# State-space exponents: the mask moved from a product of its own into the free rows of the sums' product

## The chip, the cores and the metric

The kernel runs on one core of one Trainium2 chip. The metric is the time of one execution on the device, in microseconds; the median of three runs is given with the lowest and the highest. The profiles show one execution each, with the engines TensorE (PE for the matmuls, PEld for loading their weights), VectorE (DVE), ScalarE (ACT), GpSimd (POOL) and SyncE (SP), which issues the transfers.

## The reference, cut to what matters

The program is one layer of a decoder trunk over 1024 positions of width 1024: a mixing sub-layer (stick-breaking attention beside a Mamba-2 state-space mixer), cross-attention to 256 memory rows, and a feed-forward. The change lies in the state-space mixer, in chunks of 128 positions, 4 groups of 8 heads:

```python
a_cs = jnp.cumsum(a_dt, axis=-1)
tril = jnp.tril(jnp.ones((SSM_CHUNK, SSM_CHUNK), dtype=bool))
decay = jnp.exp(jnp.where(tril, a_cs[..., :, None] - a_cs[..., None, :], -jnp.inf))
cb = jnp.einsum('bclgn,bcsgn->bcgls', cc, bc)
y_diag = jnp.einsum('bcgls,bcgels,bcsgep->bclgep', cb, decay, xc)
```

Within a chunk, position l takes from position s, at or before it, `C_l . B_s` times the exponential of the difference of two running sums. Above the diagonal the decay is zero. The states of the chunks before and a running state per group complete the output.

## The kernel before, in words

The stage in question comes behind the attention (its pools open at `with ExitStack() as p3`). It goes over 32 units, n = 0 to 31: group g = n // 8, chunk c = n % 8. Four functions handle a unit: `prep` makes its decay matrix and weighted inputs, `states` carries the running state on, `outp` forms the output and its variance, `flip` transposes it; `branch` then multiplies four finished chunks by a weight matrix. `prep` runs two units ahead of `outp`. Between them stand pieces of the memory's projections for the later cross-attention (`memory`, `mem_quanta`), which fill the first units, and `branch_load`, which splits weights. A scheduler with a model of the engines sets each engine's order when the program is built; each engine then takes its own instructions strictly in that order, waiting on semaphores. The program's rows are named by tile: `dec` is the accumulator of the exponents (two buffers), `seg` (its tile reads `s` in the profile) the decay matrix of 8 heads by 128 positions, `cb` is C B^T of four chunks.

The exponent of head h, key position s and query position l is a difference of sums, and one matmul makes it for four heads. The stationary operand is `keyrows` (128 rows by 512 positions): rows 0 to 7 and 32 to 39 hold the key-side sums of the 8 heads in two parts, rows 64 and 65 hold ones. The moving operand is `colrows` (two tiles in turn): rows 0 to 7 and 32 to 39 hold the identity over the heads, which picks each head's sum; rows 64 and 65 are loaded per unit with the query-side sums. The other 110 rows of both are zero. The mask comes from a matmul of its own into the same accumulator, ahead of it: identity times `bar`, a matrix of -2^120 above the diagonal and zero elsewhere. ScalarE then takes the exponential (L1022, two halves of four heads), and VectorE multiplies all 8 heads by C B^T (L1023, 128x1024).

The attention ends at about 1105 us of the span, and the stage's constants are made there: `identr` and `bar` by VectorE (L953, L958; the mask itself earlier by GpSimd, L956 and L957), the zeros of `colrows` and `keyrows` by GpSimd (L964), the head identities by VectorE (L967), the ones by GpSimd (L969). C B^T is computed once per four chunks in `open_four` (L995) and copied out by ScalarE (L997).

Around the change: L1045 scales the running state and L1046 adds to it; L1028 weights the inputs; L1062, L1068, L1076 and L1077 form the output; L1080 takes its variance on ScalarE, GpSimd makes 1/sqrt of it (L163, L164), and L1082 scales by it; L1095 is the transpose. L1073 is the product of the decay matrix with the inputs. L94 and L97 are the helpers that split a tensor into a high and a low part; L100 to L102 the three matmuls of a split product.

Of the kernel before, what the change touches and what calls it, by code (L numbers as in the profile page):

```python
# [8 lines left out]
F32 = mybir.dt.float32  # L9
F32R = mybir.dt.float32r  # L10
BF16 = mybir.dt.bfloat16
AF = mybir.ActivationFunctionType
ALU = mybir.AluOpType
# [3 lines left out]
P = 128  # L17
# [9 lines left out]
NG, GH = 4, 8  # L27
FFN = 2816
NF = FFN // P
ML = 256  # L30
FILL_LEFT, FILL_RIGHT = 96, 224


@with_exitstack
def hybrid_block(ctx, tc, a, out, dbg=None):
    nc = tc.nc
    V, A, G, T = nc.vector, nc.scalar, nc.gpsimd, nc.tensor

    def pool(stack, name, bufs=1, space=None, side=None):
        kw = {} if space is None else {"space": space}  # L40
        if side is not None:
            kw["side"] = side
        if space is not DRAM:
            kw["reuse_waits"] = "tile"
        return stack.enter_context(tc.tile_pool(name=name, bufs=bufs, **kw))
# [3 lines left out]
    def mk(pl, shape, dt, tag, bufs=None):  # L49
        uid[0] += 1  # L50
        kw = {} if bufs is None else {"bufs": bufs}
        return pl.tile(shape, dt, tag=tag, name=f"{tag}_{uid[0]}", **kw)
# [43 lines left out]
    def lo_of(o, i, hi, eng=V):  # L96
        eng.tensor_tensor(o, i, hi.bitcast(F32), ALU.subtract)  # L97
# [21 lines left out]
    ident = mk(cp, [P, P], F32, "ident")  # L119
# [129 lines left out]
    with ExitStack() as pa:  # L249
# [52 lines left out]
        with ExitStack() as p1:  # L302
            tt = pool(p1, "tcomb", 6)
            ep = pool(p1, "early", 4)
# [145 lines left out]
            for i, s in enumerate(steps_v + steps_z):  # L450
                if i == 4:
                    load_z()
                if i % 3 == 0 and i < 12:
                    c = i // 3
# [114 lines left out]
        with ExitStack() as p1:  # L569
# [3 lines left out]
            t4 = pool(p1, "t4b", 6)  # L573
# [144 lines left out]
        with ExitStack() as p2:  # L718
# [190 lines left out]
            for m in range(NM):  # L909
                h, half = m // 2, m % 2  # L910
                hp, r = m // 4, m % 4
# [4 lines left out]
                if m >= NM - 5:  # L916
                    n = -(-len(late) // (NM - m))
# [10 lines left out]
    with ExitStack() as p3:  # L928
        AHEAD = 2
        gb = pool(p3, "gbs", 2)  # L930
        sm = pool(p3, "smp", 2)
        t4 = pool(p3, "s4p", 3)
        t2 = pool(p3, "s2p", 9)
        ep = pool(p3, "exps", 1)
# [7 lines left out]
        def v3(t, n=HD):  # L942
            return t.rearrange("p (h d) -> p h d", d=n)
# [5 lines left out]

        identr = mk(ep, [P, P], F32R, "identr")
        V.tensor_copy(identr, ident)  # L953
        bar = mk(ep, [P, 4, P], F32R, "bar")
        tri = mk(t4, [P, GH, P], F32, "s4")
        G.memset(tri, 0.0)  # L956
        G.affine_select(tri, tri, [[0, GH], [1, P]], ALU.is_ge, -(2.0 ** 120), base=0, channel_multiplier=-1)  # L957
        V.tensor_copy(bar, tri[:, 0:4, :])  # L958
        NROW = 2
        HEADS, ONES = (0, 32), 64  # L960
        colrows = [mk(ep, [P, GH, P], F32R, f"colrows{i}") for i in range(NROW)]
        keyrows = [mk(ep, [P, HALF], F32R, f"keyrows{i}") for i in range(2)]
        for t in colrows + keyrows:
            G.memset(t.bitcast(F32), 0.0)  # L964
        for t in colrows:
            for r in HEADS:
                V.tensor_copy(t[r:r + GH], ident[r:r + GH, r:r + GH].unsqueeze(2).to_broadcast([GH, GH, P]))  # L967
        for t in keyrows:
            G.memset(t[ONES:ONES + 2].bitcast(F32), 1.0)  # L969

        def open_four(g, q):

            cols = slice(q * HALF, (q + 1) * HALF)
            d = four[g, q] = {}
            d["keys"] = keyrows[(2 * g + q) % 2]
            for j in range(2):
                nc.sync.dma_start(d["keys"][HEADS[j]:HEADS[j] + GH].bitcast(F32), key_d[j, g * GH:(g + 1) * GH, cols])
            bfm = d["bfm"] = mk(sm, [P, HALF], F32, "bfm", bufs=1)
            nc.sync.dma_start(bfm, bf_d[g][:, cols])
            cfm = d["cfm"] = mk(sm, [P, HALF], F32, "cfm", bufs=1)  # L980
            nc.sync.dma_start(cfm, cf_d[g][:, cols])
            btm = mk(sm, [P, 4, P], F32, "btm", bufs=1)
            nc.sync.dma_start(btm, bt_d[g][cols, :].rearrange("(c p) n -> p c n", p=P))
            bh = d["bh"] = mk(sm, [P, 4, P], F32R, "bh")
            bl = d["bl"] = mk(sm, [P, 4, P], F32R, "bl")
            hi_sb(bh, btm, "a")
            lo_of(bl, btm, bh)
            ch = d["ch"] = mk(sm, [P, HALF], F32R, "ch")
            cl = d["cl"] = mk(sm, [P, HALF], F32R, "cl")
            hi_sb(ch, cfm, "a")  # L990
            lo_of(cl, cfm, ch)
            pm = mk(ps, [P, 4, P], F32, "dec", bufs=2)
            for ci in range(4):
                cs = slice(ci * P, (ci + 1) * P)
                T.matmul(pm[:, ci, :], bfm[:, cs], cfm[:, cs], start=True, stop=True)  # L995
            cb = d["cb"] = mk(sm, [P, 4, P], F32, "cb")
            A.activation(cb, pm, AF.Copy)  # L997

        def prep(n):

            g, c = divmod(n, NCH)
            q, ci = divmod(c, 4)
            if c == 0:
                grp[g] = {}
            if ci == 0:
                open_four(g, q)
            f4 = four[g, q]
            cs = slice(ci * P, (ci + 1) * P)
            d = chk[n] = {}
            rows_ = slice(c * P, (c + 1) * P)  # L1010
            cr = colrows[n % NROW]
            for j in range(2):
                nc.sync.dma_start(cr[ONES + j:ONES + j + 1].bitcast(F32), sum_d[j:j + 1, g * GH:(g + 1) * GH, rows_])
            xs = d["xs"] = mk(t2, [P, HALF], F32, "s2")
            nc.sync.dma_start(xs, xs_d[g][rows_, :])
            seg = d["seg"] = mk(t4, [P, GH, P], F32, "s4")
            for j in range(2):
                hs = slice(4 * j, 4 * j + 4)
                pe = mk(ps, [P, 4, P], F32, "dec", bufs=2)
                T.matmul(pe, identr, bar, start=True, stop=False)  # L1020
                T.matmul(pe, f4["keys"][:, cs], cr[:, hs, :], start=False, stop=True)
                A.activation(seg[:, hs, :], pe, AF.Exp)  # L1022
            V.tensor_tensor(seg, seg, f4["cb"][:, ci, :].unsqueeze(1).to_broadcast([P, GH, P]), ALU.mult)  # L1023
            d["ch"], d["cl"] = f4["ch"][:, cs], f4["cl"][:, cs]
            if c < NCH - 1:
                d["bh"], d["bl"] = f4["bh"][:, ci, :], f4["bl"][:, ci, :]
                xw = mk(t2, [P, HALF], F32, "s2")
                G.tensor_tensor(v3(xw), v3(xs), bc(wm, c, g), ALU.mult)  # L1028
                xwh = d["xwh"] = mk(t2, [P, HALF], F32R, "s2r", bufs=4)
                xwl = d["xwl"] = mk(t2, [P, HALF], F32R, "s2r", bufs=4)  # L1030
                hi_sb(xwh, xw, "a")
                lo_of(xwl, xw, xwh)
# [192 lines left out]
        for n in range(AHEAD):  # L1225
            prep(n)
# [16 lines left out]
        for n in range(-AHEAD, NN + 4):  # L1243
# [15 lines left out]
            if 0 <= n - 2 < NN:  # L1259
                flip(n - 2)  # L1260
                if (n - 2) % 4 == 3:
                    g, c = divmod(n - 2, NCH)
# [24 lines left out]
    with ExitStack() as p4:  # L1287
# [15 lines left out]
        for k in range(KT):  # L1303
            oh.append(mk(op, [P, S], F32R, f"oh{k}"))
            ol.append(mk(op, [P, S], F32R, f"ol{k}"))
            for half in range(2):
                sl = slice(half * HALF, (half + 1) * HALF)
                t = mk(t2, [P, HALF], F32, "m2")
# [55 lines left out]
    t4 = pool(xt4, "t4x", 3)  # L1364
# [50 lines left out]
    with ExitStack() as q2:  # L1415
# [68 lines left out]
        for m in range(2):  # L1484
            t = mk(t4, [P, D], F32, "x4")
# [111 lines left out]
    with q6, ExitStack() as q5:  # L1597
# [37 lines left out]
        for c in range(NCH):  # L1635
            cs = slice(c * P, (c + 1) * P)
# [117 lines left out]
        for c in range(NCH):  # L1754
            cs = slice(c * P, (c + 1) * P)
# [18 lines left out]
            r = rstd_of(mss[0])  # L1774
# [36 lines left out]
```

## Time and profile before

| | |
|---|---|
| time, median of three runs | 2617.16 us (2614.66 to 2618.84) |
| the profiled execution, its own time | 2621.89 us |
| its span in the trace | 2620.1 us |
| mean granted TensorE clock | 0.99 |
| TensorE, VectorE, ScalarE, GpSimd busy | 96%, 70%, 44%, 34% of the span |
| the stage of the change | about 1105 to 1445 us of the span |
| matmuls of the mask (L1020) | 64, first start 1107.0, last 1438.4 |

In a row of the timeline the columns are the start and the duration in us, the engine, the line, the operation, what it writes and reads, and in brackets the engine's idle time before it with what ended that. A row of a table of windows gives the stretch, its length, the busy time (and count) of each engine, the granted TensorE clock, the DMA share and the rate. A row of groups gives the count, the busy time, the mean in ns, and the idle time before them with its releasers. A row of waits gives who waited for whom: total us, times, the longest.

### The profile page before, as it was taken

How to read it: one execution, taken by the hardware profiler on the slowest of the kernel's cores; microseconds unless marked ns; L12 is line 12 of the kernel's file. 1: busy time of each engine (PE TensorE's matmuls, PEld its weight loads, DVE VectorE, ACT ScalarE, POOL GpSimd, SP SyncE). 2: the span in 40 equal slices, each digit the busy share in tenths (PEclk: the TensorE clock that was granted, in tenths of full speed). 3: DMA queues.
4: the chain of work that ended last, by engine and by line, in shares of the span. 5: the costliest groups of instructions: out<-in, count | busy, mean ns of one | idle time of the engine just before them, and what ended most of it. 6: DMA issues, size and time to landing. Idle time of an engine off the chain costs nothing. (4 is left out here: it accounts for less than half of the span.)

```text
span 2620.1 us, 32774 instructions
## 1 busy us (share of the span) xinstructions
PE 2509.6 (96%) x12090; PEld 2077.3 (79%) x12090; DVE 1834.0 (70%) x2126; ACT 1152.3 (44%) x2053; POOL 887.9 (34%) x683
## 2 busy tenths in 40 slices
PE   8999999999999999989999999999999999999997
PEld 6788787787787877777888888887787888886786
DVE  7675777876689888677788654415459666666997
ACT  6433455555466655555544312314333333333342
POOL 5330544443111111254555230101114333224763
PEclk9999999999999999999999999999999999999999
DMA  6442333333322322255332461321232232324223
GB/s 226 149 137 78 120 123 105 102 105 116 101 77 61 89 73 60 96 164 179 109 90 69 135 198 68 121 67 49 81 117 72 79 95 73 97 73 153 97 109 133
DMA packets 243755, 278.02 MB, mean 106 GB/s; under 512 B 14975, under 2 KB 171272, under 8 KB 243210
## 3 DMA queue, kind: packets, MB, share of 16 engines
q1 hardware_dynamic: 243594, 275.92, 33.1%
q8 instruction: 95, 1.56, 0.2%
q14 instruction: 66, 0.54, 0.1%
HBM read 197.61 MB, written 69.87 MB: 102 GB/s over the span
## 5 line engine op out<-in xcount | busy, mean ns | idle before, releaser
L834 DVE TENSOR_TENSOR_SCAN n<-n,mask 128x128 f32<-128x128 f32 (+7 forms) x128 | 182.1, 1447 | 11.2 <-ACT n L833 8.4
L97 DVE TENSOR_TENSOR sw<-sf,sw 128x512 fp32r<-128x512 f32 x150 | 127.8, 865 | 63.9 <-ACT sw L94 63.5
L194 POOL TENSOR_TENSOR sf<-wr,wr 128x512 f32<-128x512 f32 x38 | 57.5, 1513 | 290.8 <-DMA wr<-in_w_gu_dram 104.9
L853 ACT ACTIVATE wth<-tr,mone 128x512 fp32r<-128x512 f32 x192 | 111.1, 581 | 77.2 <-PE tr L850 75.5
L94 ACT ACTIVATE sw<-sf 128x512 fp32r<-128x512 f32 x150 | 91.9, 626 | 102.6 <-PE mm L220 90.8
L854 DVE SCALAR_TENSOR_TENSOR wtl<-tr,wth 128x512 fp32r<-128x512 f32 x192 | 101.5, 546 | 39.2 <-ACT wth L853 37.9
L94 ACT ACTIVATE sw<-wr 128x512 fp32r<-128x512 f32 x113 | 71.0, 629 | 129.2 <-PE mm L220 129.0
L97 DVE TENSOR_TENSOR sw<-wr,sw 128x512 fp32r<-128x512 f32 x113 | 106.3, 943 | 29.6 <-ACT sw L94 25.3
L220 PE MATMUL mm<-h,sw 128*128 128x512 f32 x320 | 125.0, 392 | 1.8 <-DVE sw L97 1.8
L218 PE MATMUL mm<-h,sw 128*128 128x512 f32 x320 | 122.6, 391 | 2.9 <-ACT h L94 2.3
L219 PE MATMUL mm<-h,sw 128*128 128x512 f32 x320 | 125.2, 391 | 0.0
L100 PE MATMUL mm<-oth,bw 128*128 128x512 f32 (+1 forms) x320 | 121.9, 381 | 0.0
L102 PE MATMUL mm<-oth,bw 128*128 128x512 f32 (+1 forms) x320 | 119.1, 373 | 0.0
L101 PE MATMUL mm<-otl,bw 128*128 128x512 f32 (+1 forms) x320 | 118.5, 370 | 0.0
L90 POOL TENSOR_SCALAR v<-va 128x512 fp32r<-128x512 f32 x16 | 19.8, 1242 | 282.4 <-PE av L863 148.6
L602 DVE SCALAR_TENSOR_TENSOR b<-b,prmT,b 128x1023 f32<-128x1023 f32 (+2 forms) x72 | 105.7, 1468 | 12.9 <-ACT b L600 12.4
L163 POOL TENSOR_SCALAR rstd<-ms 128x1 f32<-128x1 f32 x82 | 32.6, 398 | 234.8 <-ACT x L1352 115.9
L833 ACT ACTIVATE n<-sc 128x512 f32<-128x512 f32 (+1 forms) x192 | 89.3, 487 | 49.7 <-PE sc L832 25.9
L100 PE MATMUL p<-bw,h 128*128 128x512 f32 x256 | 98.9, 391 | 3.3 <-DVE x L1354 2.3
L97 DVE TENSOR_TENSOR zl<-zr,zh 128x512 fp32r<-128x512 f32 x84 | 72.6, 878 | 40.6 <-ACT zh L94 40.5
L102 PE MATMUL p<-bw,h 128*128 128x512 f32 x256 | 100.1, 392 | 0.0
L196 POOL TENSOR_TENSOR sf<-wr 128x512 f32<-128x512 f32 x38 | 63.6, 1672 | 107.3 <-DVE sw L97 107.3
(589 smaller groups left out, 8269.0 us busy)
## 6 DMA issues: line engine op xcount, KB each, us to landing
wr<-in_w_gu_dram SPq DMA_DIRECT2D x80, 256.0 KB
wr<-in_w_in_dram SPq DMA_DIRECT2D x36, 512.0 KB
zr<-in_w_in_dram SPq DMA_DIRECT2D x32, 512.0 KB
gu_d<-t SPq DMA_DIRECT2D x44, 256.0 KB
wraw<-in_w_in_dram SPq DMA_DIRECT2D x20, 512.0 KB
xs_d<-b SPq DMA_DIRECT2D x32, 256.0 KB
s<-xs_d SPq DMA_DIRECT2D x32, 256.0 KB
s<-zs_d SPq DMA_DIRECT2D x32, 256.0 KB
```

Of the source, the lines that this page charges most:

```text
L94: A.activation(o, i, AF.Copy)
L97: eng.tensor_tensor(o, i, hi.bitcast(F32), ALU.subtract)
L100: first = T.matmul(ps, sh, mh, start=start, stop=False)
L101: T.matmul(ps, sh, ml, start=False, stop=False)
L102: T.matmul(ps, sl, mh, start=False, stop=stop)
L218: T.matmul(ps, w[0][:, k, :], b[0][:, k, :], start=first and k == 0, stop=False, skip_group_check=True)
L219: T.matmul(ps, w[0][:, k, :], b[1][:, k, :], start=False, stop=False, skip_group_check=True)
L220: T.matmul(ps, w[1][:, k, :], b[0][:, k, :], start=False, stop=last and k == 3, skip_group_check=True)
L602: V.scalar_tensor_tensor(acc[:, sh:], y[:, :S - sh], cw(3 - sh, f), acc[:, sh:], ALU.mult, ALU.add)
L834: V.tensor_tensor_scan(nt[:, 0:L][:, ::-1], nt[:, 0:L][:, ::-1], mask[:, S - L:][:, ::-1], 1.0, ALU.mult, ALU.max)
L853: A.activation(wh[:, t0 * P:], pt[:, t0 * P:], AF.Identity, bias=mone)
L854: V.scalar_tensor_tensor(wl[:, t0 * P:], pt[:, t0 * P:], -1.0, wh[:, t0 * P:].bitcast(F32), ALU.add, ALU.subtract)
```

## The change

The mask's own matmul goes. Its work is put into the 110 rows that were zero. Row k of `keyrows` now holds 1 for positions s > k, and row k of `colrows` holds -2^120 in column l = k, for each head. Their product adds -2^120 exactly where s > l. Eighteen rows belong to the sums, so the mask of these 18 columns is put into the row n further on (8 for the heads' rows, 2 for the ones): for these columns some positions just above the diagonal stay unmasked, and the exponential there can be large or infinite. So C B^T is set to zero above the diagonal by GpSimd, once per four chunks, and VectorE's product first takes the minimum of the decay and 3.0e38, so that no infinity meets a zero.

The constants `identr` and `bar` and the clearing memsets go; VectorE fills `colrows` (two products of 128x1024 and six small ones) and copies a triangle of ones, made by GpSimd, into `keyrows`.

```diff
+BIG, FAR = 3.0e38, -(2.0 ** 120)
...
-        identr = mk(ep, [P, P], F32R, "identr")
-        V.tensor_copy(identr, ident)
-        bar = mk(ep, [P, 4, P], F32R, "bar")
-        tri = mk(t4, [P, GH, P], F32, "s4")
-        G.memset(tri, 0.0)
-        G.affine_select(tri, tri, [[0, GH], [1, P]], ALU.is_ge, -(2.0 ** 120), base=0, channel_multiplier=-1)
-        V.tensor_copy(bar, tri[:, 0:4, :])
...
-        for t in colrows + keyrows:
-            G.memset(t.bitcast(F32), 0.0)
         for t in colrows:
+            V.tensor_scalar(t, ident.unsqueeze(1).to_broadcast([P, GH, P]), FAR, None, ALU.mult)
+            for r, n in ((0, GH), (32, GH), (ONES, 2)):
+                V.tensor_scalar(t[:, :, r:r + n], ident[:, r + n:r + n + 1].unsqueeze(1).to_broadcast([P, GH, n]), FAR, None, ALU.mult)
             for r in HEADS:
                 V.tensor_copy(t[r:r + GH], ident[r:r + GH, r:r + GH].unsqueeze(2).to_broadcast([GH, GH, P]))
+        u = mk(sm, [P, 4, P], F32, "cb")
+        G.memset(u, 1.0)
+        G.affine_select(u, u, [[0, 4], [1, P]], ALU.is_gt, 0.0, base=0, channel_multiplier=-1)
         for t in keyrows:
+            V.tensor_copy(t, u.rearrange("p c i -> p (c i)"))
             G.memset(t[ONES:ONES + 2].bitcast(F32), 1.0)
...
             A.activation(cb, pm, AF.Copy)
+            G.affine_select(cb, cb, [[0, 4], [1, P]], ALU.is_ge, 0.0, base=0, channel_multiplier=-1)
...
-                T.matmul(pe, identr, bar, start=True, stop=False)
-                T.matmul(pe, f4["keys"][:, cs], cr[:, hs, :], start=False, stop=True)
+                T.matmul(pe, f4["keys"][:, cs], cr[:, hs, :], start=True, stop=True)
                 A.activation(seg[:, hs, :], pe, AF.Exp)
-            V.tensor_tensor(seg, seg, f4["cb"][:, ci, :].unsqueeze(1).to_broadcast([P, GH, P]), ALU.mult)
+            V.scalar_tensor_tensor(seg, seg, BIG, f4["cb"][:, ci, :].unsqueeze(1).to_broadcast([P, GH, P]), ALU.min, ALU.mult)
```

The order that the scheduler makes moves only within this stage. VectorE at the stage's entry, before (the last attention weights, L854, then the constants; `oT` is the attention's last output, `bl` and `s2r` low parts):

```order
L854 SCALAR_TENSOR_TENSOR wtl_10030<-tr_10027,wth_10029 128x128
L953 CAST identr_10103<-ident_86 128x128
L958 CAST bar_10105<-s_2053_10106 128x512
L871 TENSOR_TENSOR oT_9787<-av_9975,gt_10050 64x512
L967 CAST colrows_2054_10112<-ident_86 8x1024 x2
L967 CAST colrows_2055_10113<-ident_86 8x1024 x2
L97 TENSOR_TENSOR bl_10558<-btm_10555,bh_10557 128x512
```

and in the changed kernel (line numbers are those of the changed file):

```order
L855 SCALAR_TENSOR_TENSOR wtl_10030<-tr_10027,wth_10029 128x128
L958 TENSOR_SCALAR colrows_2051_10103<-ident_86 128x1024
L958 TENSOR_SCALAR colrows_2052_10104<-ident_86 128x1024
L967 CAST keyrows_2053_10105<-cb_10119 128x512
L967 CAST keyrows_2054_10106<-cb_10119 128x512
L872 TENSOR_TENSOR oT_9787<-av_9975,gt_10050 64x512
L960 TENSOR_SCALAR colrows_2051_10103<-ident_86 128x8x8 x2
L960 TENSOR_SCALAR colrows_2051_10103<-ident_86 128x8x2
L960 TENSOR_SCALAR colrows_2052_10104<-ident_86 128x8x8 x2
L960 TENSOR_SCALAR colrows_2052_10104<-ident_86 128x8x2
L98 TENSOR_TENSOR bl_10551<-btm_10548,bh_10550 128x512
L962 CAST colrows_2051_10103<-ident_86 8x1024 x2
```

Ten instructions take the place of two, and the head identities now come behind `bl`.

TensorE in the steady part of the stage, before (`mm` is a branch product):

```order
L1020 MATMUL dec_12470<-bar_10105,identr_10103 128x512
L1021 MATMUL dec_12470<-colrows_2054_10112,keyrows_2057_10115 128x512
L1020 MATMUL dec_12474<-bar_10105,identr_10103 128x512
L1021 MATMUL dec_12474<-colrows_2054_10112,keyrows_2057_10115 128x512
L100 MATMUL mm_12485<-oth_11951,bw_11980 128x512
```

and in the changed kernel, at the same unit:

```order
L1094 MATMUL ptr_12420<-ident_86,s_2551_12167 128x128 x4
L1020 MATMUL dec_12432<-colrows_2051_10103,keyrows_2054_10106 128x512
L1020 MATMUL dec_12435<-colrows_2051_10103,keyrows_2054_10106 128x512
L101 MATMUL mm_12445<-oth_11922,bw_11949 128x512
```

Two matmuls per unit are gone and their neighbours have closed up.

GpSimd at the entry, in the changed kernel; the second select of C B^T stands ahead of a running-state product (L1044) and, four rows on, a variance chain (L164, L165):

```order
L164 TENSOR_SCALAR rstd_10409<-ms_10407 128x1
L165 TENSOR_TENSOR rstd_10409<-rstd_10409,mhalf_93 128x1
L997 AFFINE_SELECT cb_10563<-cb_10563 128x512
L1044 TENSOR_TENSOR state_10720<-state_10603,cdm_2482 128x512
L1067 TENSOR_TENSOR s_2180_10630<-s_2180_10630,s_2182_10636 128x512
L1027 TENSOR_TENSOR s_2196_10697<-s_2192_10687,wm_2481 128x512
L1061 TENSOR_TENSOR s_2208_10749<-s_2130_10436,dsk_92 128x512
L164 TENSOR_SCALAR rstd_10521<-ms_10519 128x1
```

Before, none of these rows was a select.

## The prediction

> **What bounds the kernel now.** I read the page's busy times first, then the table of windows over the state-space stage (1105 to 1445 us of the span), then TensorE's instructions in order of time, then VectorE's and GpSimd's at the stage's entry.
>
> ```profile
> span 2620.1 us, 32774 instructions
> PE 2509.6 (96%) x12090; PEld 2077.3 (79%) x12090; DVE 1834.0 (70%) x2126; ACT 1152.3 (44%) x2053; POOL 887.9 (34%) x683
> ...
> core 0: us, PE busy (x) PEld busy (x) DVE busy (x) ACT busy (x) POOL busy (x), PEclk, DMA share, GB/s
> 1105.00:1165.00 60.00, 45.92 (x275) 39.39 (x275) 51.64 (x60) 36.31 (x64) 38.61 (x32) 0.89 0.54 162
> 1165.00:1240.00 75.00, 69.89 (x392) 59.92 (x391) 52.82 (x58) 43.38 (x76) 29.02 (x29) 0.98 0.59 187
> 1240.00:1445.00 205.00, 205.00 (x1125) 175.71 (x1124) 167.49 (x205) 104.43 (x202) 115.84 (x110) 1.00 0.30 90
> ```
>
> The average of 96% hides three stretches. From 1240 on TensorE is busy 205.00 of 205.00 us: it is the bound, and VectorE has 37.5 us of idle time beside it. From 1105 to 1165 TensorE stands still 14.1 us and VectorE only 8.4: the entry goes by VectorE and by waits. From 1165 to 1240 TensorE misses 5.1 us. The same windows for the removed product's line alone (TensorE columns first) say how many of its 64 matmuls lie where:
>
> ```profile
> 1105.00:1165.00 60.00, 7.00 (x14) 2.90 (x14) 0.89 0.54 162
> 1165.00:1240.00 75.00, 4.25 (x10) 2.03 (x10) 0.98 0.59 187
> 1240.00:1445.00 205.00, 17.89 (x40) 7.60 (x40) 1.00 0.30 90
> ```
>
> Their busy time, 29.1 us, is not what they cost: matmuls overlap in the records. The cost is the distance between starts, in the full stretch:
>
> ```profile
> 1296.91 0.48 PE L1020 MATMUL dec<-bar,identr 128*128 128x512 f32 x1
> 1297.22 0.40 PE L1021 MATMUL dec<-colrows,keyrows 128*128 128x512 f32 x1
> 1297.46 0.40 PE L1020 MATMUL dec<-bar,identr 128*128 128x512 f32 x1
> 1297.69 0.40 PE L1021 MATMUL dec<-colrows,keyrows 128*128 128x512 f32 x1
> 1297.93 0.39 PE L100 MATMUL mm<-oth,bw 128*128 128x512 f32 x1
> ```
>
> 0.23 us from start to start (1297.46 to 1297.69). The first L1020 takes 0.31 because it comes behind transposes; with it gone, L1021 stands there and takes the 0.31, so each removal is worth 0.23, not 0.40 to 0.48.
>
> **The change part by part.** *The product on TensorE.* 40 matmuls lie where TensorE never waits: 40 x 0.23 = 9.2 us off the end, provided the others keep up. 10 lie in the middle, where it is busy 93%; memory weights arrive there late, so a part of the gain turns into waiting: 10 x 0.23 = 2.3 at most, 0 at least, I take half, 1.15. 14 lie at the entry: at most 3.2 us, 0 at least; only the stretches without waits pay, I take a third, 1.05. Sum 11.4; bounds 9.2 and 14.7.
>
> *The setup.* Before, GpSimd cleared the rows and VectorE made the two constants:
>
> ```profile
> 1105.24 0.22 DVE L953 CAST identr<-ident 128x128 fp32r<-128x128 f32 x1
> 1105.37 0.42 DVE L958 CAST bar<-s 128x512 fp32r<-128x512 f32 x1
> 1107.09 3.79 DVE L967 CAST colrows<-ident 8x1024 fp32r<-8x1024 f32 x4
> 1110.91 1.42 DVE L97 TENSOR_TENSOR bl<-btm,bh 128x512 fp32r<-128x512 f32 x1
> ...
> 1122.61 1.28 DVE L1147 SCALAR_TENSOR_TENSOR wraw<-wraw,rstd,bw 128x1024 f32<-128x1024 f32 x1 [0.46 <-POOL rstd L164]
> 1137.45 1.21 DVE L97 TENSOR_TENSOR bw<-wraw,bw 128x1024 fp32r<-128x1024 f32 x1
> ```
>
> Now VectorE does it, in its queue ahead of everything of the stage: two scalar products of 128x1024, two copies of 128x512, six small products; the four casts of 3.79 stay. The copies are the form of L958, 0.42 each, 0.84. The 128x1024 product is not in the trace in this form: twice the 0.42 cast bounds it below at 0.8, the 1.21 tensor-tensor above; it reads one tensor as the cast does, so I take 0.8, twice 1.6. The small ones lie below the 0.22 of the 128x128 cast; 0.15 each, 0.9. Less the two casts that go (0.13 + 0.42): 1.6 + 0.84 + 0.9 - 0.55 = **2.8 us** later, at most 4.0. VectorE then runs nearly without a gap to 1150, and the products that wait on these rows feed it, so I let it count in full.
>
> *The product with C B^T* becomes a scalar-tensor-tensor. The nearest pair at 128x1024 is 1.28 against 1.21: 0.07 more, 32 times 2.2 us on VectorE, 20 of them (1.4 us; their row stands under C) inside its 37.5 us of idle time after 1240. The other 12 make 0.84 before that, where the engine is full for about half of the time; I count 0.4. Below: no difference. Infinities or a minimum have no row; I take them to cost nothing.
>
> *GpSimd.* Rows for what goes and comes, the select and its memset first:
>
> ```profile
> 1081.20 0.95 POOL L956 MEMSET s<- 128x1024 f32 x1 [15.97 <-PE sc L832]
> 1082.23 2.73 POOL L957 TENSOR_SCALAR_AFFINE_SELECT s<-s 128x1024 f32<-128x1024 f32 x1
> ...
> 1105.44 1.24 POOL L964 MEMSET colrows<- 128x1024 f32 x1 [2.52 <-DVE wtl L854]
> 1106.63 0.99 POOL L964 MEMSET keyrows<- 128x512 f32 x2
> 1107.67 1.96 POOL L969 MEMSET keyrows<- 2x512 f32 x2
> ```
>
> A 128x512 select is half of 2.73: 1.37 us, eight of them 10.9. Four come after 1240 (one per four chunks): 5.5 us on an engine that is busy 115.84 of 205, and the select and the product that reads it stand two units ahead of the matmuls that need them; a unit there lasts about 10 us (205 us hold 20 of the products), so they cost nothing. If that cover were gone, each would hold one VectorE product by 1.37. At the entry the memsets save as much as the first select costs; the second stands in the queue ahead of the variance chains, which the entry already waits for:
>
> ```profile
> 1107.60 0.63 PE L100 MATMUL pst<-s2r,bh 128*128 128x512 f32 x1
> 1108.03 0.63 PE L101 MATMUL pst<-s2r,bh 128*128 128x512 f32 x1
> ...
> 1113.59 0.49 PE L101 MATMUL po<-stl,ch 128*128 128x512 f32 x1 [1.72 <-DVE stl L97]
> ...
> 1132.82 0.77 PE L1095 MATMUL ptr<-ident,s 128*128 128x128 f32 x4 [3.86 <-ACT s L1082]
> ...
> 1146.70 1.12 PE L1095 MATMUL ptr<-ident,s 128*128 128x128 f32 x4 [4.84 <-ACT s L1082]
> ...
> ACT s L1082 <- POOL rstd L164: 15.0, 9, 3.9
> ```
>
> TensorE's two longest waits end with ScalarE's L1082, and that with GpSimd's rstd. A select in between costs 0 to 1.37; I take 0.5. The SyncE queue issues the same transfers; the key rows' transfer now waits for the copies instead of the memsets, both near 1108.
>
> What is late next: the first exponent product needs the casts of the first column rows. By the sum of VectorE's rows these end near 1111.9 (1105.3 + 1.6 + 0.84 + 0.6 for oT + 0.9 + 0.7 for bl + 1.9); before, that product could start at 1111.0. Now the second chunk's state product, which stood ahead of it, is queued behind it. That lies inside the 2.8.
>
> One rule speaks against the size. The Trainium skill, TensorE: Matmul & The Clock Gate, section Back-to-back issue gap, gives about 131 ns per 512-column matmul in a sustained stream. By it the 40 would be an estimated 5.2 us and not 9.2. The trace does not agree: 0.23 us, at a granted clock of 1.00.
>
> **Sum.** -9.2 - 1.15 - 1.05 + 2.8 + 0.4 + 0.5 = **-7.7 us**. The span goes from 2620.1 to 2612.4. The profiled execution took 2621.89 us in all, 4.73 above the median of the runs, 2617.16; against that median the forecast is **2609.5 us**.
>
> **The rivals.** *B, the entry fills up.* All 64 removals count (14.7) and the setup falls into waits that are there anyway: 2617.16 - 14.7 = 2602.5. For it: 19.2 us of TensorE's standing still before 1240, where late work could be taken in. Against: VectorE is the busy one there, and it gets more work.
>
> *C, VectorE hands half back.* After 1240 it has 167.49 + 1.4 of work; with TensorE at 195.8 us that is 86%, and in-order waits could cost TensorE half of the 9.2. With nothing from the middle and the entry: -4.6 + 2.8 + 0.4 + 0.5 = -0.9, so 2616.3. For it, these rows of VectorE's groups in that window:
>
> ```profile
> L1023 DVE TENSOR_TENSOR s<-s,cb 128x1024 f32<-128x1024 f32 x20 | 28.6, 1428 | 6.3 <-ACT s L1022 6.3
> ...
> L1076 DVE TENSOR_TENSOR s<-s,pd 128x512 f32<-128x512 f32 x20 | 13.6, 680 | 11.9 <-POOL s L1068 9.5 <-PE pd L1073 2.4
> ```
>
> The product takes 1.43 on average, against 1.21 for a product of that length alone: it is held up by GpSimd's work, and waits for it elsewhere (9.5). Four selects add 5.5 if each held VectorE for its whole length: 174.4 of 195.8, 89%. Still not full, so half is the worst I see. The Trainium skill, SBUF — State Buffer, section SBUF: two separate sides, has the port pair of VectorE and GpSimd as an exclusive lock for the whole instruction; that is the full 5.5, and the stretched products agree with it.
>
> *D, the entry loses more than the rest gains: slower.* One mechanism: in-order queues pass the later setup on. VectorE 4.0 late; two selects at full length, 2.7, in front of the variance chains; each of three long waits then leaves TensorE at half pace (0.43 us between the starts at 1107.60 and 1108.03, against 0.23) for some 3.4 us more, 1.7 lost each, 5.1; and the memory products, which fill the waits up to 1240, come late, so that the 5.1 us missed there double. Sum 4.0 + 2.7 + 5.1 + 5.1 - 9.2 = +7.7: 2624.9. It decides where the entry loses over 9.2. For it: 0.89 granted clock there already. Against: up to the last of the memory's normalised rows VectorE has the same instructions as before, but for the setup and one more addition.
>
> That the product is not really gone is excluded by the order below: the row is missing at both exponents.
>
> **How the numbers follow.** Forecast A (2605 to 2613.5) 0.50, B 0.20, C 0.20, D 0.10. A measurement of this kernel tells some 0.2% (5.2 us: 2611.9 to 2622.4) from no change. Faster: 0.44 of A, all of B, 0.02 of C: 0.66. Same: 0.06 + 0.18 + 0.02 of D: 0.26. Slower: 0.08. The range reaches into B and C: 2601.5 to 2617; D and B's far end are left out.
>
> **What would show it.** Right: the window from the same place on holds no L1020 of the old kind, TensorE stays at full busy time, and the stretch is 8 to 9 us shorter; VectorE's busy share there rises from 82% to 85 to 88%; the minimum-product's shortest is 1.2 to 1.3; a select takes 1.3 to 1.5; the first exponent product starts 1 us later than 1111.0. Wrong: idle TensorE after 1240 with a VectorE or GpSimd releaser (C); a clock under 0.89 and longer waits for L1082's successor (D); the setup's 128x1024 products over 1.3; or a stretch shorter by over 12.

## The result, and the profile after

The changed kernel takes 2612.12 us (median of 14 runs, 2605.31 to 2617.03); the kernel before, on the same chip, 2616.94 us (14 runs, 2613.59 to 2619.67). The ratio is 0.9982, with a 95% interval of 0.9974 to 0.9990: a gain of 4.7 us, between 2.6 and 6.8. Two later comparisons on other chips gave 0.9980 and 0.9981. The interval lies below 1, so the change is faster. But the gain is a small one: 2612.12 us lies just inside the band of 2611.9 to 2622.4 that the prediction counts as no change, to which it gave a chance of 0.26, against 0.66 for faster. The forecast was a gain of 7.7 us.

The page's first lines after the change:

```profile
span 2607.9 us, 32662 instructions
PE 2498.9 (96%) x12026; PEld 2069.1 (79%) x12026; DVE 1831.2 (70%) x2134; ACT 1149.1 (44%) x2053; POOL 884.3 (34%) x687
```

The span is 12.2 us shorter than that of before, but this difference must not be read as the change's. To see that, I take four marks from VectorE's timeline: the attention's last instruction (`wtl`), the tenth and the last of the 32 transposed outputs (`otl`), and the first instruction of the stage behind (`m`). The kernel before:

```profile
1105.04 0.28 DVE L854 SCALAR_TENSOR_TENSOR wtl<-tr,wth 128x128 fp32r<-128x128 f32 x1
1268.49 0.69 DVE L1099 TENSOR_TENSOR otl<-ptr,oth 128x512 fp32r<-128x512 f32 x1
...
1477.75 0.69 DVE L1099 TENSOR_TENSOR otl<-ptr,oth 128x512 fp32r<-128x512 f32 x1 [0.38 <-ACT oth L1098]
...
1516.40 0.69 DVE L1326 TENSOR_TENSOR m<-m,mm 128x512 f32<-128x512 f32 x1 [1.46 <-PE mm L102]
```

and the changed kernel:

```profile
1096.95 0.28 DVE L855 SCALAR_TENSOR_TENSOR wtl<-tr,wth 128x128 fp32r<-128x128 f32 x1
1263.56 0.69 DVE L1098 TENSOR_TENSOR otl<-ptr,oth 128x512 fp32r<-128x512 f32 x1
...
1463.84 0.69 DVE L1098 TENSOR_TENSOR otl<-ptr,oth 128x512 fp32r<-128x512 f32 x1 [0.38 <-ACT oth L1097]
...
1503.75 0.69 DVE L1325 TENSOR_TENSOR m<-m,mm 128x512 f32<-128x512 f32 x1 [0.29 <-PE mm L103]
```

8.1 of the 12.2 us (1105.04 to 1096.95) lie ahead of that `wtl`, where TensorE runs the same 5245 matmuls in both kernels. Over the 14 profiles of this study the attention's end lay anywhere from 1097 to 1105 us, and two profiles of the unchanged kernel before had it at 1105.3 and 1099.1. So all later readings count from the end of that `wtl`, and the stage falls into three pieces. "Entry" runs from there to the tenth `otl`, "stretch" from the tenth to the last, "handover" from the last to the first `m`. Before: 163.2, 209.3 and 38.7 us. After: 166.3, 200.3 and 39.9 us. (The entry is 1268.49 less 1105.32, and so on.) The stretch gained 9.0 us and the entry lost 3.2.

The tenth `otl` comes some 28 us behind the place from which the prediction counted its 40 products, so not all of them lie in the stretch. The windows of entry and stretch in the kernel before, for the mask's product alone (TensorE columns first):

```profile
1105.32:1268.49 163.17, 13.95 (x30) 6.07 (x30) 0.95 0.51 159
1268.49:1477.75 209.26, 15.19 (x34) 6.46 (x34) 1.00 0.29 87
```

And the stretch with all instructions, of the kernel before and then of the changed one:

```profile
1268.49:1477.75 209.26, 209.26 (x1139) 178.92 (x1139) 166.31 (x211) 99.16 (x192) 106.86 (x105) 1.00 0.29 87
```

```profile
1263.56:1463.84 200.28, 200.28 (x1099) 171.29 (x1098) 164.10 (x210) 98.19 (x192) 108.00 (x109) 1.00 0.30 90
```

The stretch held 34 of the mask's products, yet TensorE has 40 matmuls less in it: six others are done ahead of the mark in the changed kernel's order. The two pieces thus exchange work, and the price of a matmul has to be taken from TensorE's count: 9.0 us for 40, 0.225 us each.

The windows of the stage, shifted by the 8 us, with the columns of the windows before:

```profile
1097.00:1157.00 60.00, 45.60 (x275) 39.34 (x276) 54.17 (x69) 36.95 (x66) 38.33 (x34) 0.86 0.54 163
1157.00:1232.00 75.00, 65.90 (x360) 55.60 (x359) 51.18 (x54) 41.11 (x73) 26.88 (x26) 0.95 0.56 178
1232.00:1432.00 200.00, 200.00 (x1097) 171.37 (x1096) 163.39 (x204) 102.92 (x203) 117.90 (x117) 1.00 0.31 92
```

From 1232 on TensorE is again busy without a gap, and VectorE at 163.39 of 200 us, 82% as before. Ahead of that TensorE misses 14.4 us in the first window (14.1 before) and 9.1 in the second (5.1 before). The loss is in the middle, where nothing of the setup runs.

The rows by line, with count, shortest, median and longest in ns: the new product, the selects, and the setup. First the product of the kernel before, then the changed kernel's lines:

```profile
L1023 DVE TENSOR_TENSOR s<-s,cb x32: 1207/1222/2309, 1114.9 to 1444.2; 128x1024 f32<-128x1024 f32 x32
```

```profile
L1022 DVE SCALAR_TENSOR_TENSOR s<-s,cb x32: 1206/1224/2314, 1105.8 to 1433.2; 128x1024 f32<-128x1024 f32 x32
L997 POOL TENSOR_SCALAR_AFFINE_SELECT cb<-cb x8: 629/636/1192, 1101.2 to 1401.1; 128x512 f32<-128x512 f32 x8
L958 DVE TENSOR_SCALAR colrows<-ident x2: 684/685/686, 1097.1 to 1097.7; 128x1024 fp32r<-128x1024 f32 x2
```

The minimum in the product costs nothing (1206 and 1224 ns against 1207 and 1222). A select takes 0.63 us, and a fill 0.685. The setup on VectorE's timeline, and the first exponent product on TensorE's:

```profile
1097.15 1.28 DVE L958 TENSOR_SCALAR colrows<-ident 128x1024 fp32r<-128x1024 f32 x2
1098.35 0.76 DVE L967 CAST keyrows<-cb 128x512 fp32r<-128x512 f32 x2
...
1099.85 0.66 DVE L960 TENSOR_SCALAR colrows<-ident 128x64 fp32r<-128x64 f32 x6
```

```profile
1104.00 0.93 PE L1020 MATMUL dec<-colrows,keyrows 128*128 128x512 f32 x2 [4.74 <-DVE colrows L962]
```

The new setup is 1.28 + 0.76 + 0.66 = 2.70 us, less the 0.55 that went: 2.15 us. The first exponent product with the sums starts 6.8 us behind the attention's end (5.7 before).

### The profile page after: what moved, and what is told of

Same layout as the page of the kernel before. It is cut to its first block, busy times and chain, and to the rows that moved or that the text cites. A ratio compares the mean times of both kernels' runs of the same rounds, so it can differ in the third digit from the quotient of the medians.

```text
span 2607.9 us, 32662 instructions
## 1 busy us (share of the span) xinstructions
PE 2498.9 (96%) x12026; PEld 2069.1 (79%) x12026; DVE 1831.2 (70%) x2134; ACT 1149.1 (44%) x2053; POOL 884.3 (34%) x687
## 5 line engine op out<-in xcount | busy, mean ns | idle before, releaser
L854 ACT ACTIVATE wth<-tr,mone 128x512 fp32r<-128x512 f32 x192 | 110.9, 580 | 75.5 <-PE tr L851 73.8
L603 DVE SCALAR_TENSOR_TENSOR b<-b,prmT,b 128x1023 f32<-128x1023 f32 (+2 forms) x72 | 106.3, 1477 | 12.0 <-ACT b L601 11.4
L164 POOL TENSOR_SCALAR rstd<-ms 128x1 f32<-128x1 f32 x82 | 29.1, 355 | 239.8 <-ACT x L1351 116.4
L834 ACT ACTIVATE n<-sc 128x512 f32<-128x512 f32 (+1 forms) x192 | 89.1, 486 | 47.9 <-PE sc L833 23.9
```

The lines of the kernel that those rows point to most:

```text
L603: V.scalar_tensor_tensor(acc[:, sh:], y[:, :S - sh], cw(3 - sh, f), acc[:, sh:], ALU.mult, ALU.add)
L854: A.activation(wh[:, t0 * P:], pt[:, t0 * P:], AF.Identity, bias=mone)
```

## The experiments

Two theories went into them. The first is the prediction's own: each removed product gives 0.23 us wherever TensorE has no gap, and the entry pays the price of the setup on VectorE, since its queue passes every delay on. The second: the first is right for the stretch, but the entry is set by the order that the scheduler makes, which every edit changes at many places, and not by the price of the instructions added. The first theory then wants an entry that is late whenever the setup is paid; the second wants entries that scatter among kernels of equal work.

### The mask's product left out, without the new setup

```diff
-                V.tensor_copy(t[r:r + GH], ident[r:r + GH, r:r + GH].unsqueeze(2)...)
+                V.tensor_copy(t[r:r + GH], ident[r:r + GH, 64:64 + GH].unsqueeze(2)...)
...
-            G.memset(t[ONES:ONES + 2].bitcast(F32), 1.0)
+            G.memset(t[ONES:ONES + 2].bitcast(F32), 0.0)
...
-                T.matmul(pe, identr, bar, start=True, stop=False)
-                T.matmul(pe, f4["keys"][:, cs], cr[:, hs, :], start=False, stop=True)
+                T.matmul(pe, f4["keys"][:, cs], cr[:, hs, :], start=True, stop=True)
```

(an edit of the kernel before)

> The kernel before without the mask's product, and nothing else of the change: its setup, its two constants and its product with C B^T stay. The mask is left out, and the head rows and the ones are zero so that all exponents are zero and stay finite; every other instruction is as before. Theory 1: the full stretch is 9.2 us shorter as with the whole change, the entry loses nothing and may gain up to 3; with 1 given back at the handover, 8 to 12 us faster. Theory 2 (the entry loses because the queues' order there is reshuffled by any change, not by the new setup): 9.2 less some 3 at the entry again, 4 to 6 us faster, like the whole change.

Measured: 2611.89 us, ratio 0.9968 (0.9957 to 0.9979). Entry 158.6, stretch 200.6, handover 41.3 us. The stretch is 8.7 us shorter than before, with 38 matmuls less (1101 in TensorE's count), almost as in the changed kernel, so the gain there is the products' alone; neither the minimum nor the selects take anything of it. The entry is 4.6 us shorter than in the profile before, and 7.8 shorter than in that of the change. By the ratio the gain is 8.4 us, which the first theory wanted, by the medians 5.7, which the second wanted. The entry, with 30 products less, gained, where the second theory wanted a loss of some 3. So this run by itself fits the first theory better; the next one does not.

### The changed kernel with the mask's product put back

```diff
+        identr = mk(ep, [P, P], F32R, "identr")
+        V.tensor_copy(identr, ident)
+        bar = mk(ep, [P, 4, P], F32R, "bar")
+        tri = mk(t4, [P, GH, P], F32, "s4")
+        G.memset(tri, 0.0)
+        G.affine_select(tri, tri, [[0, GH], [1, P]], ALU.is_ge, -(2.0 ** 120), base=0, channel_multiplier=-1)
+        V.tensor_copy(bar, tri[:, 0:4, :])
...
-                T.matmul(pe, f4["keys"][:, cs], cr[:, hs, :], start=True, stop=True)
+                T.matmul(pe, identr, bar, start=True, stop=False)
+                T.matmul(pe, f4["keys"][:, cs], cr[:, hs, :], start=False, stop=True)
```

> The changed kernel with the mask's own product put back beside the free rows (identity times the same constant, made as before): setup, selects and the minimum are paid for, the 64 matmuls are not saved. Theory 1: 2 to 5 us slower than before, all of it before the full stretch. Theory 2: as a matter of order it can come out between 3 faster and 6 slower, with no tie to the setup's 2.1 us more on VectorE.

Measured: 2614.69 us, ratio 0.9990 (0.9981 to 0.9999). This kernel has all 64 products of before and on top the whole new setup, the selects and the minimum, and it is not slower, where the first theory wanted 2 to 5 us. Its marks:

```profile
1098.19 0.28 DVE L855 SCALAR_TENSOR_TENSOR wtl<-tr,wth 128x128 fp32r<-128x128 f32 x1
1256.41 0.69 DVE L1106 TENSOR_TENSOR otl<-ptr,oth 128x512 fp32r<-128x512 f32 x1
...
1465.70 0.69 DVE L1106 TENSOR_TENSOR otl<-ptr,oth 128x512 fp32r<-128x512 f32 x1 [0.38 <-ACT oth L1105]
```

Entry 157.9, stretch 209.3 us. The stretch is back to that of before, as both theories wanted, and so is TensorE's count in it, 1139. The entry is 5.2 us *shorter* than in the first profile of the kernel before and 3.5 shorter than in its second (below), with as many matmuls and more instructions on VectorE and GpSimd. The first theory, which has the entry pay for the setup, falls here.

### The mask's product twice

```diff
                 T.matmul(pe, identr, bar, start=True, stop=False)
+                T.matmul(pe, identr, bar, start=False, stop=False)
```

> The kernel before with the mask's product issued twice (the exponents above the diagonal get twice -2^120, the output stays the same). Theory 1: 40 products more in the full stretch at 0.23 us, 9.2 us, and 0 to 5.5 of the 24 others: 9 to 15 us slower. Rival (the spare time of the weight loads hides a product whose weights never change, so one more costs 0.13 us): 5 to 8 us slower.

Measured: 2628.89 us, ratio 1.0043 (1.0031 to 1.0055), 11.4 us slower. Entry 163.3, stretch 217.4, handover 41.2 us. The stretch is 8.1 us longer, for 36 more matmuls in TensorE's count (1175), 34 of them the mask's. TensorE's timeline in it:

```profile
1296.47 0.40 PE L1021 MATMUL dec<-bar,identr 128*128 128x512 f32 x1
1296.71 0.40 PE L1022 MATMUL dec<-colrows,keyrows 128*128 128x512 f32 x1
1296.94 0.40 PE L1020 MATMUL dec<-bar,identr 128*128 128x512 f32 x1
```

From start to start 0.24 and 0.23 us. A matmul added in the stretch costs as much as one taken away gives, 0.225 us each. The total of 11.4 us lies in the range of the first theory; the rival, 5 to 8 us, falls.

### The same kernels again

The changed kernel was run unchanged twice more, and the kernel before once, for the scatter of the three pieces.

> The changed kernel once more, for the spread of its inner times. Theory 1 (the full stretch pays 0.23 us a product, the entry and the handover to the next stage lose): from the attention's end to the next stage's first product it is 4.6 us shorter than before in this profile too, within 1 us; the median is 3 to 7 us under that of before. Theory 2 (the entry's loss of 3.2 us is a matter of one execution, transfers landing by chance): the inner time moves by 2 us or more between the two profiles of the same kernel.

> The changed kernel beside the variants on one chip: the tenth unit 2 to 4 us later than before, 3 to 7 us faster in all, by either theory.

> The kernel before once more, for its inner times. Both theories: from the attention's end to the next stage's first addition 411 us, within 1 of the first profile; a difference of over 2 would take away the ground from all comparisons of single profiles.

Measured, the changed kernel: 2613.35 us, ratio 0.9980 (0.9971 to 0.9988), and 2611.40 us, ratio 0.9981 (0.9971 to 0.9992). Entry 165.7 and 167.3, stretch 200.1 and 200.0, handover 39.9 and 37.8. The kernel before, a single execution: 2612.95 us; entry 161.5, stretch 209.3, handover 38.1. So a repeated entry moves by 1.6 to 1.7 us, a repeated stretch by 0.3 at most, a repeated handover by 2.1.

All three pieces together are 411.1 and 408.8 us before, and 406.5, 405.8 and 405.1 after. The two profiles of the kernel before lie 2.3 apart. That is more than the 1 expected, and more than the 2 that was named beforehand as taking the ground from comparisons of single profiles. So below, a difference between single profiles says something only where it is well over 2.3 us, and the ratios of the runs stand beside it. By the means, the change makes the entry 4.1 us longer (162.3 to 166.4), the stretch 9.1 shorter, and the handover 0.9 longer, which is within its own scatter. Together 4.1 us shorter, as the runs' 4.7. The tenth unit of the changed kernel's third profile, expected 2 to 4 us later than before, came 4.1 to 5.8 later.

### The same instructions in other orders

Two edits of the changed kernel only move lines in the program's text. No instruction is added or taken away. The first puts the triangle and the key rows ahead of the column rows, the second the first two memory pieces ahead of the first two `prep`.

```diff
+        u = mk(sm, [P, 4, P], F32, "cb")
...
+            G.memset(t[ONES:ONES + 2].bitcast(F32), 1.0)
         for t in colrows:
...
-        u = mk(sm, [P, 4, P], F32, "cb")
...
-            G.memset(t[ONES:ONES + 2].bitcast(F32), 1.0)
```

```diff
+        for m in range(2):
+            memory(m)
         for n in range(AHEAD):
             prep(n)
-        for m in range(2):
-            memory(m)
```

> The changed kernel with the key rows' setup written ahead of the column rows' setup: the same instructions, another order at the entry. Theory 1 (the entry loses by the setup's price): the tenth unit 2 to 4 us later than before, as in the changed kernel, and 3 to 7 us faster in all. Theory 2 (the entry goes by the order that the scheduler makes): the tenth unit anywhere from 6 us earlier to 6 later than before, most likely over 2 us away from the changed kernel's; behind it the same 9 us gain in both.

> The changed kernel with the memory's two normalised halves written ahead of the first two units: the same instructions, another order. Theory 1: as the changed kernel at the tenth unit, within 1.5 us. Theory 2: over 2 us away from it, to either side; behind it the same 9 us gain.

Measured: key rows first 2608.93 us, ratio 0.9963 (0.9948 to 0.9977), entry 159.1, stretch 201.8, handover 40.3. Memory first 2608.84 us, ratio 0.9972 (0.9956 to 0.9987), entry 163.6, stretch 200.6, handover 39.5. The same instructions take 159.1, 163.6 or 166.4 us for the entry. A part of the 7.3 us between them is matmuls that an order moves across the mark: TensorE's count in the entry is 788, 793 and 796. Entry and stretch together are free of that, 360.9, 364.2 and 366.6 us: 5.7 us apart, where repeats of one kernel differ by 1.7 at most. With the keys first the difference is clear of the scatter, and the second theory holds there: another order of the same instructions changes the entry. With the memory first it is 2.4 us, about the scatter, and the interval of its ratio takes in the changed kernel's. The changed kernel was not profiled on the chip of these two; one fill, below, was, and its entries there and on another chip differ by 0.9 us only. With the keys first, the gain over the kernel before is 9.7 us by the ratio (6.0 to 13.6) and 7.8 by the medians, where 7.7 was forecast.

The granted clock alone does not explain it. The windows of the entry with the keys first:

```profile
1101.00:1161.00 60.00, 43.65 (x251) 38.05 (x251) 54.68 (x67) 33.73 (x62) 37.84 (x33) 0.80 0.49 148
1161.00:1236.00 75.00, 70.47 (x412) 60.87 (x411) 57.10 (x64) 47.42 (x84) 34.27 (x32) 1.00 0.66 208
```

The granted clock is 0.80 in the first window, below the 0.86 of the changed kernel, and TensorE even less busy; yet in the second it misses 4.5 us, not 9.1. What goes along with the early entries is a shorter wait for the memory's weights (`wraw` by transfer, split by ScalarE and VectorE into `bw`), read from the waits over the first 140 us of the stage (total, times, longest). Before:

```profile
DVE bw L97 <- ACT bw L94: 22.9, 8, 8.0
ACT bw L94 <- DMA wraw<-in_w_xkv_dram: 15.1, 9, 4.0
```

the changed kernel:

```profile
DVE bw L98 <- ACT bw L95: 25.4, 12, 6.3
ACT bw L95 <- DMA wraw<-in_w_xkv_dram: 24.6, 14, 4.4
```

with the mask's product put back:

```profile
DVE bw L98 <- ACT bw L95: 12.7, 8, 3.0
ACT bw L95 <- DMA wraw<-in_w_xkv_dram: 11.9, 5, 3.2
```

and with the keys first:

```profile
DVE bw L98 <- ACT bw L95: 14.5, 8, 3.8
ACT bw L95 <- DMA wraw<-in_w_xkv_dram: 11.1, 10, 3.2
```

VectorE's two shortest waits (12.7 and 14.5) belong to two of the three shortest entries (157.9 and 159.1; the third, 158.6 without the mask's product, had 18.5), the longest (23.9 to 25.4 over its three profiles) to the changed kernel, the latest. The second row of each pair, the wait for the transfer itself, does not go along so well: with one fill (below) it is 23.9 and 21.9 us, nearly the changed kernel's, at entries of 160.3 and 159.4. That is a reading, not a proof: no run changed these weights' transfers alone.

### Cheaper setups

Three edits of the changed kernel, in four runs, take work from VectorE in the setup: the second column tile copied from the first by ScalarE (run twice), the same with the keys first, and the head identities written by ScalarE.

```diff
-        for t in colrows:
+        for t in colrows[0:1]:
...
+        A.activation(colrows[1], colrows[0].bitcast(F32), AF.Copy)
```

```diff
-                V.tensor_copy(t[r:r + GH], ident[r:r + GH, r:r + GH].unsqueeze(2).to_broadcast([GH, GH, P]))
+                A.activation(t[r:r + GH], ident[r:r + GH, r:r + GH].unsqueeze(2).to_broadcast([GH, GH, P]), AF.Copy)
```

> The changed kernel with the second column tile copied from the finished first by ScalarE (one ACTIVATE of 128x1024, about 1.05 us) in place of VectorE's six instructions for it: VectorE has some 3.0 us less at the entry (0.64, 0.33 and two casts of 1.0). Theory 1: the entry gains up to 3 us on the changed kernel, 6 to 9 us faster than before in all. Theory 2: no such tie; the tenth unit is anywhere from 6 earlier to 6 later than before.

> The one fill once more, in the same comparison as the changed kernel. Both theories: 0.2% to 0.5% under the kernel before, its inner time from the attention's end within 1.5 us of its first profile.

> Both edits at once: the key rows' setup written first, and the second column tile copied by ScalarE. Theory 1 (the setup's price on VectorE): their gains add, the tenth unit 5 us or more earlier than in the changed kernel, as with the one fill alone. Theory 2 (the order): the two gains of 5 to 7 us each at the tenth unit do not add; anywhere from 3 earlier to 9 earlier than the changed kernel's, 4 to 11 us faster than before in all.

> The changed kernel with the four head identities made by ScalarE instead of VectorE, which has 4.0 us less to do at the entry. Theory 1: at least as much gained at the tenth unit as by the one fill (which took 3.0 from VectorE and came out 5 us earlier than the changed kernel). Theory 2: no tie to the 4.0; it may come out later than the changed kernel's tenth unit in spite of it.

Measured, with the pieces of all kernels side by side (means where a kernel has more than one profile):

| kernel | median us | ratio to before (95%) | entry | stretch | handover | all three |
|---|---|---|---|---|---|---|
| before (2 profiles) | 2616.94 | | 162.3 | 209.3 | 38.4 | 409.9 |
| changed (3) | 2612.12 | 0.9982 (0.9974 to 0.9990) | 166.4 | 200.1 | 39.2 | 405.8 |
| one fill | 2609.01 | 0.9960 (0.9946 to 0.9975) | 160.3 | 200.9 | 38.4 | 399.6 |
| one fill, again | 2607.22 | 0.9961 (0.9948 to 0.9975) | 159.4 | 200.7 | 38.9 | 399.0 |
| one fill, keys first | 2609.38 | 0.9971 (0.9959 to 0.9982) | 162.9 | 201.3 | 38.3 | 402.5 |
| heads by ScalarE | 2609.62 | 0.9969 (0.9959 to 0.9979) | 161.3 | 200.6 | 40.1 | 401.9 |

One fill has the lowest ratios of the study, 0.4% below before on two chips (keys first, 0.9963, lies within their intervals), and is 6.5 us shorter through the stage than the changed kernel. But it does not gain by an earlier start, which the first theory would have. The first exponent product of this kernel:

```profile
1115.67 1.05 PE L1021 MATMUL dec<-colrows,keyrows 128*128 128x512 f32 x2
```

The attention ended at 1103.62 here, so it starts 12.0 us behind it (12.0 in the repeat as well), 5.2 us *later* than in the changed kernel, and still the tenth unit is 6 us earlier. And the two edits that each help by themselves, one fill and keys first, do not add up: together 162.9, against 160.3 and 159.1 alone. The first theory wanted 5 us or more of the two together, and 3.5 came; it wanted the heads by ScalarE, with 4.0 us less on VectorE, to gain at least as much as one fill with 3.0 less, and 5.1 came against 6.1 and 7.0. So the savings on VectorE do not size these gains. Whether they are a part of them is open: all three lighter setups come out ahead of the changed kernel, but so do the kernels that only reorder and the one with the mask's product put back, which save VectorE nothing. The changed kernel's order has the longest entry of all that were run.

## Why the prediction was right or wrong, point by point

**The products of the full stretch** (-9.2): right in mechanism and price. Between the tenth and the last unit the stretch is 9.1 us shorter with 40 matmuls less, 8.7 with 38 less where the products alone are left out, the same with them put back, and 8.1 longer with 36 more: 0.225 to 0.23 us each, the 0.23 from start to start. That 9.1 meets the term's 9.2 is a coincidence of the mark, though. Only 34 of the 40 products of the term lie behind it, worth some 7.7 us; the rest are the six matmuls that went over to the entry. The Trainium skill's rule (TensorE: Matmul & The Clock Gate, section Back-to-back issue gap), about 131 ns each, does not fit: by it the 40 would be an estimated 5.2 us, and the trace gives 9.1, at a granted clock of 1.00.

**C, VectorE hands half back**: did not happen. TensorE stays at 200.00 of 200 us, and VectorE's groups behind it (same columns as before) read:

```profile
L1022 DVE SCALAR_TENSOR_TENSOR s<-s,cb 128x1024 f32<-128x1024 f32 x19 | 26.4, 1388 | 7.8 <-ACT s L1021 6.0 <-POOL s L1067 1.8
...
L1075 DVE TENSOR_TENSOR s<-s,pd 128x512 f32<-128x512 f32 x19 | 12.9, 681 | 11.3 <-POOL s L1067 9.4 <-PE pd L1072 1.8
```

The product's mean is 1.39 us, not longer than the 1.43 of before, and the wait for GpSimd is the same 9.4 to 9.5. My sign that VectorE's share would rise to 85 to 88% failed: it stayed at 82% between the windows at the same place, and went from 79.5% to 81.9% of the stretch between the tenth and the last unit, since the minimum costs nothing and the selects half of what I took.

**The prices of single instructions.** The fill, 0.685 us, lies below the lower bound of 0.8 (twice the 128x512 cast), so the setup cost 2.15 and not 2.8. The minimum, under 0.01 and not 0.07. The select, 0.63 and not 1.37: the row of 2.73 was no measure, for VectorE was at work beside most of it (the select runs from 1082.23 to 1084.96).

```profile
1081.77 2.29 DVE L834 TENSOR_TENSOR_SCAN n<-n,mask 128x1024 f32<-128x1024 f32 x1 [0.94 <-ACT n L833]
```

A 128x128 select of the same kernel takes 0.29 us; by this and the 0.63, one of 128x1024 would take an estimated 1.1. That the scan held the select up is not shown, only that it lay beside it. All three errors were on the safe side, and all three are small beside the next point.

**The entry** (-1.15 - 1.05 + 2.8 + 0.4 + 0.5 = +1.5): the step that failed. Measured +4.1 by the means (2.5 to 5.8 between single profiles). The mark shifts both figures alike: six of the stretch term's products belong to this piece, 1.4 us, and the six matmuls that moved in cost about as much. So 2.6 of the 3.6 us by which the three pieces (-4.1) fell short of the forecast lie here. The rest is the handover, +0.9, which the sum did not have and which scatters by 2.1 in one kernel. What failed is not the size of a term but the way from the setup to the end, "I let it count in full". The first exponent product did start 1 us later, as worked out; but that start does not set the entry. With one fill it is 5 us later still and the tenth unit is 6 us earlier. With the mask's product put back on top of the new setup, the entry is the shortest of all. The same instructions in three orders give 360.9, 364.2 and 366.6 us for entry and stretch. The term that should have stood there is one for the order: some 6 us between the orders tried, of unknown sign, in a stage whose first 135 us go by waits. How much of the 1.15 and the 1.05 for the early products came, no run tells apart.

**D, the entry loses more than the rest gains**: the entry did lose, but 4.1 us and not 16.9, and the whole was not slower. D's signs came: a clock of 0.86 in the first window, and runs of 16 matmuls at half pace behind a wait. Such a run in the entry of the kernel before, and then of the changed one:

```profile
1121.22 1.89 PE L1073 MATMUL pd<-s,s 128*128 128x96 f32 x16
```

```profile
1127.17 3.67 PE L1072 MATMUL pd<-s,s 128*128 128x96 f32 x16 [0.74 <-DVE s L1075]
```

But a clock of 0.80 went with one of the earliest entries, so that sign says nothing about the end. **B, the entry fills up**, did not happen in the changed kernel. Other orders go a part of that way: 0.9963 with the keys first and 0.9960 with one fill, where that rival has 0.9944.

**The forecast**, 2609.5 us, was 2.6 us below the measured median, and the range held it. Against the kernel before, the gain of 7.7 lies outside the measured 2.6 to 6.8. The direction came from the stretch, as worked out; that the entry did not take more of it was luck of the order, since the sum had no measure for that.

What stays open: which of the order's many differences sets the entry. VectorE's waits for the memory's weights go along with it in most kernels, but no run moved them alone; nor was it tested whether such an edit also moves the tiles' places in memory, and whether that has a part.

## What to carry to other kernels

In a stretch where TensorE shows no gap, price a removed or added product by the distance between starts, not by its busy time, and count TensorE's matmuls between the marks instead of assuming them: with that count, three edits agree within 0.01 us per matmul. In a stretch that goes by waits, and whose order a scheduler makes, an edit's own price says little; measure how far the same instructions in another order move it, and set that as the uncertainty of the forecast. And count time from a mark just ahead of the edit: of 12 us between two spans, 8 had nothing to do with the change.

## What was not expected of the hardware

A fill of 128x1024 took 0.685 us in the changed kernel and about 1.06 in the kernel with the keys first (2.11 for two), where GpSimd's writing of the ones rows lies beside them. First VectorE, then GpSimd, in the kernel with the keys first:

```profile
1102.35 2.11 DVE L964 TENSOR_SCALAR colrows<-ident 128x1024 fp32r<-128x1024 f32 x2
```

```profile
1102.16 1.75 POOL L962 MEMSET keyrows<- 2x512 f32 x2 [5.03 <-DVE keyrows L961]
```

The two fills took 2.11 us instead of 1.28, and the two memsets 1.75 instead of the 1.13 that they take in the changed kernel. Both engines together needed 2.30 us (1102.16 to 1104.46), where the times in the changed kernel add up to 2.41: about as long as if they had worked in turn, not side by side. The Trainium skill (SBUF — State Buffer, section SBUF: two separate sides) has it that GpSimd and VectorE, in some of its forms, share a port pair which one of them takes for a whole instruction while the other is blocked; this trace agrees.
